# A transformer block on one core: constants issued after the first block's weights, and one pair of weight sums placed behind a block inverse's copies

## The chip, the core and the metric

The kernel runs on one core of a Trainium2 chip. The time is the device time of one execution in microseconds (us); the kernel before has a median of 1452.83 over three runs. A core has engines that work side by side, each in its own order: TensorE (PE in the profile; its weight loads are PEld), VectorE (DVE), ScalarE (ACT), GpSimd (POOL) and SyncE (SP), which here issues loads. Engines wait for one another and for DMA transfers through semaphores.

## The reference

One block of a transformer on x of 256 tokens by 2048:

```python
proj = x @ w_in                                    # 2048 x 11864, split into 12 parts
qkv_a = causal_short_conv(qkv_a, conv_w)           # width 4, then silu
log_decay = -exp(a_log) * softplus(a_in + dt_bias)
o_a = gated_delta_rule_chunked(q_a, k_a, v_a, log_decay, sigmoid(b_in))   # chunks of 64 tokens, triangular solves
o_a = o_a * rsqrt(mean(o_a**2)) * gdn_norm_w * silu(z)
o_b = dsa_sparse_attention(q_b, k_b, v_b, q_i, k_i, w_i, rel_bias)        # top 64 keys by an index score
merged = sigmoid(gate_a) * (o_a @ w_branch_a) + sigmoid(gate_b) * (o_b @ w_branch_b)
x = layer_norm(alpha * x + merged @ w_out)
x = layer_norm(alpha * x + (silu(x @ w_gate) * (x @ w_up)) @ w_ffn_out)
```

## The kernel before

Each float is split into a part hi, rounded to the matmul's format, and a remainder lo, and a product of two floats takes three matmuls (hi by hi, hi by lo, lo by hi). Nearly all of the time is TensorE's work on weights. A weight comes in a chunk of 128 x 1024 floats: `chunk()` (lines 85 to 94) has SP issue the load into `raw` (line 89), ScalarE round it to `hi` (line 91) and VectorE subtract to get `lo` (line 93). `raw`, `hi` and `lo` have four buffers each.

The first block (the loop above line 456) reads x and `win` in eight steps, with a piece of `ws` after every second step (line 454). After the sixth step SP also issued the constants: `ident` and `cp` (an identity matrix, masks and tables; lines 458 and 459), and in a loop (line 462) `cw` (the convolution's taps), `alog`, `dtb`, two parts of `oneh` (shown as s_e, whose memory it shares) and `gnw`. `cw` is first used by the taps of line 480 (ScalarE) and line 482 (VectorE), `cp` and `ident` by products on lines 517 and 521.

Then `wws` is multiplied in groups of four chunks (`group_ws`, lines 153 and 156). After every chunk a clock ticks, and each tick lets chains, which are Python generators, write one more step of other work. TensorE and SP run in exactly this written order. On VectorE, ScalarE and GpSimd a scheduler sets the order when the program is built, from priorities (chunks go ahead by 70 places, `high_priority(offset=lead)`) and the length of the work; when it runs, each engine takes its list strictly from the front.

Two chains matter here. The **block inverse** (`merge`, lines 590 to 640, called for growing blocks) inverts the triangular matrices of the delta rule: products on TensorE (line 606), a copy of each out of PSUM into `s_ak` (VectorE line 610, ScalarE line 612), four groups of four transposes (line 617), each copied into `s_t`, alternately by ScalarE (line 623, groups 0 and 2) and VectorE (line 621, groups 1 and 3), and then products of the two (line 631), which VectorE adds or copies into `s_u` (lines 636 and 638). PSUM has four banks for these small results (`aux`). The **kept pairs** (`kept_chain`) prepare sums of feed-forward weights long before they are needed: for each of four pairs SP issues two loads of 512 KB (line 950), VectorE makes four sums in place (`four_sums`: lines 934, 935, 938, 939), ScalarE casts them to hi (line 960, tile k_hi), VectorE subtracts (line 961), and GpSimd writes both to memory (lines 963 and 964). They have a low priority (`-LEAD`). The pairs alternate between two places, shown as k_rawoh (first and third pair) and k_raws_x (second and fourth); all share one hi buffer. The other work around 200 us is the index score of the sparse attention: ScalarE's relu (line 807, tile rel), VectorE's weighted sums (lines 813 and 815, tile sc), and the search for the largest 64 (lines 822 and 823).

Of the kernel before, what the change touches and what calls it, by code (L numbers as in the profile page):

```python
# [8 lines left out]
F32 = mybir.dt.float32  # L9
# [3 lines left out]
OP = mybir.AluOpType  # L13
# [4 lines left out]
P = 128  # L18
# [14 lines left out]
LEAD = 70  # L33
# [25 lines left out]
C_ID, C_TRI, C_ONE, C_M1, C_M2, C_M3, C_LV, C_SH = 0, 128, 256, 384, 512, 640, 768, 960  # L59
# [4 lines left out]
def block_kernel(ctx: ExitStack, tc: tile.TileContext, xT, x, cpack, onehot, relb, convw, alog, dtb, gnw,  # L64
                 ws, wws, win, wz, wgt, wba, wbb, woa, wob, wfi, wfg, wfo, ln1g, ln1b, ln2g, ln2b, out):
    nc = tc.nc
# [3 lines left out]
    sm = ctx.enter_context(tc.tile_pool(name="sm", bufs=1, side="left"))  # L70
# [4 lines left out]
    def ps_aux():  # L75
        return aux.tile([P, 512], F32, name="aux", tag="aux")
# [4 lines left out]
    ident = cst.tile([P, P], F32, name="ident")  # L81
# [18 lines left out]
    def start(gen, at_once=False):  # L100
        chains.append([gen, clock[0] + (next(gen) if at_once else 0)])
# [17 lines left out]
    def event(name):  # L119
        done[name] = clock[0]  # L120
# [86 lines left out]
    def split(hi, lo, src):  # L207
        nc.scalar.copy(hi, src)
        nc.vector.tensor_sub(lo, src, hi.bitcast(F32))
# [131 lines left out]
    def T(name, shape, dtype=F32, tag=None):  # L341
        return p1.tile(shape, dtype, name=name, tag=tag or name)
# [23 lines left out]
    cp = T("cp", [P, C_N - P])  # L366
    alog_t = T("alog", [P, H])
    dtb_t = T("dtb", [P, H])
    cw = T("cw", [P, 24, 4])
    gnw_t = T("gnw", [P, 1])  # L370
    oneh = s_e.rearrange("p a h d -> p (a h d)")
# [6 lines left out]
    def t16(name):  # L378
        return T(name, [P, NTB, H])
# [46 lines left out]
    def first_chunk(src):  # L426
        raw, hi, lo = (wp.tile([P, 512], d, name=n, tag=n) for n, d in (("raw", F32), ("hi", F32R), ("lo", F32R)))
        hv = [slice(c * S, (c + 1) * S) for c in range(2)]
        for h in hv:
            nc.sync.dma_start(raw[:, h], src[:, h])  # L430
        for c, h in enumerate(hv):
            split(hi[:, h], lo[:, h], raw[:, h])
            ws_mm([pss[c]], hi[:, h], lo[:, h], 0, KT, xh, xl, 2)

    for i in range(8):
        k0 = 2 * i
        parts = [srcs[i]] if i > 2 else [srcs[i][:, :512], srcs[i][:, 512:]]
        for j, src in enumerate(parts):
            k, n = k0 + j, 2 // len(parts)
            xr = xraw[k // 8][:, k % 8:k % 8 + n, :]  # L440
            xp = XH[k // 4][:, k % 4:k % 4 + n], XL[k // 4][:, k % 4:k % 4 + n]
            if i:
                nc.sync.dma_start(xr, xT[:, k:k + n, :])
            if k == 0:
                nc.vector.tensor_copy(xp[0], xr)
                nc.vector.tensor_sub(xp[1], xr, xp[0].bitcast(F32))
                first_chunk(src)
            else:
                split(*xp, xr)
                hi, lo = chunk(src, lead=0)  # L450
                ws_mm(pss, hi, lo, k, KT, xh, xl, 4)
        if i % 2:
            ww = slice((i - 1) * 256, (i + 1) * 256)
            nc.sync.dma_start(wsr[:, ww], ws[i // 2])
            split(wsh[:, ww], wsl[:, ww], wsr[:, ww])
            ws_mm([pk], wsh[:, ww], wsl[:, ww], k0 - 2, KT, xh, xl, 1)
        if i == 5:
            nc.sync.dma_start(ident, cpack[:, C_ID:C_ID + P])
            nc.sync.dma_start(cp, cpack[:, P:])
            for dst, src in ((cw, convw), (alog_t, alog), (dtb_t, dtb), (oneh[:32, :384], onehot),  # L460
                             (oneh[:32, 384:392], relb), (gnw_t, gnw)):
                nc.sync.dma_start(dst, src)

    smT = T("smT", [P, S])
    nc.scalar.copy(smT, pk[:, :S])
# [118 lines left out]

    rk2, rk, nb, nbe, rkb = t16("rk2"), t16("rk"), t16("nb"), t16("nbe"), t16("rkb")
    rq2, rq, fo = t16("rq2"), t16("rq"), t16("fo")
    d_m = dr.tile([4, NTB * H, 32, 32], F32, name="d_m")
    d_x = dr.tile([4, NTB * H, 32, 32], F32, name="d_x")

    def merge(b):  # L590

        n = P // (2 * b)
        hi = (64, P) if n == 1 else (0, P)
        w = 64 if n == 1 else 96
        uv = s_u.rearrange("p t (n two b) -> p t n two b", two=2, b=b)
        if n == 1:
            mp, up = mnv[:, :, 0:64], s_u[:, :, 0:64]
        else:
            mp = s_sq.rearrange("p (t c) -> p t c", c=64)
            up = s_e.rearrange("p a h d -> p (a h d)")[:, 0:1024].rearrange("p (t c) -> p t c", c=64)  # L600
            nc.scalar.copy(up.rearrange("p t (n b) -> p t n b", n=n), uv[:, :, :, 0, :])
        for q in range(2):
            a = ps_aux()
            for i in range(8):
                t = q * 8 + i
                nc.tensor.matmul(a[0:64, i * 64:(i + 1) * 64], mp[hi[0]:hi[1], t, :], uv[hi[0]:hi[1], t, :, 1, :],
                                 start=True, stop=True)
            dst = s_ak[0:64, q * 512:(q + 1) * 512]
            if q % 2:
                nc.vector.tensor_copy(dst, a[0:64])  # L610
            else:
                nc.scalar.copy(dst, a[0:64])
                yield 1
        for q in range(4):
            a = ps_aux()
            for i in range(4):
                nc.tensor.transpose(a[0:64, i * w:(i + 1) * w], up[0:w, q * 4 + i, :], ident[0:w, 0:w])
            dst = s_t[0:64, q * 4:q * 4 + 4, 0:w]
            src = a[0:64, 0:4 * w].rearrange("p (t d) -> p t d", t=4)
            if q % 2:  # L620
                nc.vector.tensor_copy(dst, src)
            else:
                nc.scalar.copy(dst, src)
            if q == 1:
                yield 1
        yield 2
        for q in range(2):
            a = ps_aux()
            for i in range(8):
                t = q * 8 + i  # L630
                nc.tensor.matmul(a[0:w, i * 64:(i + 1) * 64], s_t[0:64, t, 0:w], s_ak[0:64, t * 64:(t + 1) * 64],
                                 start=True, stop=True)
            dst = uv[0:w, q * 8:q * 8 + 8, :, 1, :]
            src = a[0:w].rearrange("p (t n b) -> p t n b", t=8, b=b)
            if n == 1:
                nc.vector.tensor_copy(dst, src)
            else:
                nc.vector.tensor_tensor(dst, src, dst, op=OP.add)
            yield 1 if q == 0 else 3


    def key_chain():
# [54 lines left out]
        yield "qc1s"  # L697
        yield from merge(32)
        yield from merge(64)
        event("inv")  # L700

# [225 lines left out]

    d_s = dr.tile([len(KEPT), 2, P, 2, 1024], F32, name="d_s")

    def four_sums(ra, rb, lead=0):  # L930

        r0, r1, s0, s1 = (t[:, n * 512:n * 512 + 512] for t in (ra, rb) for n in range(2))
        with tc.high_priority(offset=lead):
            nc.vector.tensor_add(r0, r0, s1)
            nc.vector.tensor_add(s1, r1, s1)
        yield 1
        with tc.high_priority(offset=lead):
            nc.vector.tensor_add(r1, r0, r1)
            nc.vector.tensor_add(s0, r1, s0)

    def kept_chain(ms, wait, old, old_hi, gap, ev):
        yield wait
        raws = [T(f"k_raw{t}", [P, 2, 1024], tag=t) for t in old]
        hi = T(f"k_hi{old_hi}", [P, 2, 1024], F32R, tag=old_hi)
        for m in ms:
            if gap and m > ms[0]:
                yield gap
            raw = raws[m % len(old)]
            for i in range(2):
                nc.sync.dma_start(raw[:, i], wfg[KEPT[m] - 1, i])  # L950
                yield 1
            yield 1
            for _ in four_sums(raw[:, 0], raw[:, 1], -LEAD):
                yield 1
            yield 1
            for i in range(2):
                with tc.high_priority(offset=-LEAD):
                    for n in range(2):
                        cs = slice(n * 512, n * 512 + 512)
                        nc.scalar.copy(hi[:, i, cs], raw[:, i, cs])  # L960
                        nc.vector.tensor_sub(raw[:, i, cs].bitcast(F32R), raw[:, i, cs], hi[:, i, cs].bitcast(F32))
                yield 1
                nc.gpsimd.dma_start(d_s[m, 0, :, i], hi[:, i].bitcast(F32))
                nc.gpsimd.dma_start(d_s[m, 1, :, i], raw[:, i])
        event(ev)

    start(kept_chain(range(4), KEPT_FROM, ("oh_", "s_x"), "ol_", 0, "kept0"))
    conv_first(s_kT, pss)
    event("kc0")
# [646 lines left out]
    for j in (1, 2, 3):  # L1616
        nc.vector.scalar_tensor_tensor(v1[j], v1[j], mv[:, 0:1], gt2[:, slice(j * 512, j * 512 + 512)],
                                       op0=OP.subtract, op1=OP.mult)
    for j in (1, 2, 3):
        nc.vector.scalar_tensor_tensor(v1[j], v1[j], rs, bt2[:, slice(j * 512, j * 512 + 512)],  # L1620
                                       op0=OP.mult, op1=OP.add)
# [113 lines left out]
```

## Time and profile before

| What | us |
|---|---|
| Median of three runs (1451.66 to 1455.95) | 1452.83 |
| The profiled execution | 1453.58 |
| its span in the trace | 1451.8 |
| TensorE busy in it | 1443.1 |
| VectorE busy | 1283.2 |
| ScalarE busy | 816.6 |

The difference between the profiled execution's time and its span, 1.78 us, lies around the span. A row of a timeline gives the start, the duration, the engine, the line of the kernel, the operation, what it writes and reads, its shape and how many stand together, and in brackets the idle time of the engine just before it and what ended that. A row of the waits gives engine, tile and line, what was waited for, and the total, the number and the longest wait. Times in both are us from the start of the span.

### The profile page before, as it was taken

How to read it: one execution, taken by the hardware profiler on the slowest of the kernel's cores; microseconds unless marked ns; L12 is line 12 of the kernel's file. 1: busy time of each engine (PE TensorE's matmuls, PEld its weight loads, DVE VectorE, ACT ScalarE, POOL GpSimd, SP SyncE). 2: the span in 40 equal slices, each digit the busy share in tenths (PEclk: the TensorE clock that was granted, in tenths of full speed). 3: DMA queues.
4: the chain of work that ended last, by engine and by line, in shares of the span. 5: the costliest groups of instructions: out<-in, count | busy, mean ns of one | idle time of the engine just before them, and what ended most of it. 6: DMA issues, size and time to landing. Idle time of an engine off the chain costs nothing.

```text
span 1451.8 us, 19648 instructions
## 1 busy us (share of the span) xinstructions
PE 1443.1 (99%) x7137; PEld 1214.2 (84%) x7137; DVE 1283.2 (88%) x1769; ACT 816.6 (56%) x1025; POOL 58.3 (4%) x79
## 2 busy tenths in 40 slices
PE   9999999999999999999999999999999999999998
PEld 8888888888888888888888888888888888888886
DVE  6798988789799969998897899999999998989987
ACT  5765454557556646655445565656566565554552
POOL 0001011121000000000000000000000000000000
PEclk9999999999999999999999999999999999999999
DMA  8656589854456775766865777677766666888863
GB/s 290 196 162 196 174 213 335 287 188 159 171 202 221 264 248 201 249 186 208 296 210 202 244 263 281 244 267 257 279 214 211 213 218 247 313 338 269 318 210 116
DMA packets 102833, 339.81 MB, mean 234 GB/s; under 512 B 17792, under 2 KB 18984, under 8 KB 102224
## 3 DMA queue, kind: packets, MB, share of 16 engines
q1 hardware_dynamic: 88800, 311.35, 62.1%
q0 software_dynamic: 6752, 24.85, 5.0%
q10 hardware_dynamic: 7184, 2.36, 0.7%
q8 instruction: 56, 0.92, 0.3%
q14 instruction: 41, 0.34, 0.1%
HBM read 314.19 MB, written 24.31 MB: 233 GB/s over the span
## 4 chain that ended last, share of the span: by engine, by line
PE 98%; DMA 1%; ACT 0%; DVE 0%; issue 0%; POOLq 0%; SPq 0%; ACTq 0%; DVEq 0%
PE acc L217 11%; PE acc L218 11%; PE acc L219 11%; PE acc L153 10%; PE aux L217 10%; PE aux L219 10%; PE aux L218 10%; PE acc L156 5%; PE acc L173 4%; PE acc L175 4%; PE acc L174 4%; PE aux L174 2%; PE aux L175 2%; PE aux L173 1%; PE aux L737 1%; DMA k_rawoh__2366<-in_wfg_dram 1%
## 5 line engine op out<-in xcount | busy, mean ns | idle before, releaser
L91 ACT CAST hi<-raw 128x1024 fp32r<-128x1024 f32 (+1 forms) x384 | 392.9, 1033 | 326.7 <-PE acc L219 71.7
L93 DVE TENSOR_TENSOR lo<-raw,hi 128x1024 fp32r<-128x1024 f32 (+1 forms) x384 | 458.9, 1205 | 82.4 <-ACT hi L91 78.4
L153 PE MATMUL acc<-X,hi 128*128 128x512 f32 x640 | 203.7, 400 | 0.0
L217 PE MATMUL acc<-hi,X 128*128 128x512 f32 x370 | 145.2, 392 | 0.0
L219 PE MATMUL acc<-hi,X 128*128 128x512 f32 x370 | 144.1, 389 | 0.0
L218 PE MATMUL acc<-lo,X 128*128 128x512 f32 x370 | 144.0, 389 | 0.0
L156 PEld LDWEIGHTS acc<-X,lo 128*128 128x128 f32 x640 | 120.2, 188 | 28.3
L156 PE MATMUL acc<-X,lo 128*128 128x256 f32 x640 | 126.0, 278 | 0.0
L217 PE MATMUL aux<-hi,X 128*128 128x512 f32 x306 | 119.7, 391 | 0.0
L219 PE MATMUL aux<-hi,X 128*128 128x512 f32 x306 | 119.2, 389 | 0.0
L218 PE MATMUL aux<-lo,X 128*128 128x512 f32 x306 | 119.1, 389 | 0.0
L153 PEld LDWEIGHTS acc<-X,hi 128*128 128x128 f32 x640 | 97.5, 189 | 2.0 <-ACT hi L91 0.7
L241 ACT CAST f_thi<-f_wt 128x1024 fp32r<-128x1024 f32 x60 | 63.2, 1053 | 59.7 <-DVE f_wt L246 23.8
L219 PEld LDWEIGHTS acc<-hi,X 128*128 128x128 f32 x370 | 69.4, 188 | 14.5
L217 PEld LDWEIGHTS acc<-hi,X 128*128 128x128 f32 x370 | 69.5, 188 | 14.3 <-ACT s_u L979 0.4
L218 PEld LDWEIGHTS acc<-lo,X 128*128 128x128 f32 x370 | 69.5, 188 | 14.0
L242 DVE TENSOR_TENSOR f_tlo<-f_wt,f_thi 128x1024 fp32r<-128x1024 f32 x60 | 73.1, 1219 | 7.2 <-ACT f_thi L241 7.0
L219 PEld LDWEIGHTS aux<-hi,X 128*128 128x128 f32 x306 | 57.4, 188 | 12.0
L218 PEld LDWEIGHTS aux<-lo,X 128*128 128x128 f32 x306 | 57.5, 188 | 11.9
L217 PEld LDWEIGHTS aux<-hi,X 128*128 128x128 f32 x306 | 57.4, 188 | 11.7
L173 PE MATMUL acc<-hi,X 128*128 128x512 f32 x160 | 64.3, 402 | 0.0
L241 ACT CAST thi<-wt 128x1024 fp32r<-128x1024 f32 x36 | 37.9, 1053 | 46.2 <-DVE wt L246 29.6
(661 smaller groups left out, 3145.1 us busy)
## 6 DMA issues: line engine op xcount, KB each, us to landing
raw<-in_wfg_dram SPq DMA_DIRECT2D x125, 512.0 KB, 5.1
raw<-in_wws_dram SPq DMA_DIRECT2D x80, 512.0 KB, 4.2
raw<-in_wfo_dram SPq DMA_DIRECT2D x70, 512.0 KB, 5.1
raw<-in_wgt_dram SPq DMA_DIRECT2D x49, 512.0 KB, 3.7
f_wraw<-in_wfg_dram SPq DMA_DIRECT2D x30, 512.0 KB, 6.5
raw<-in_win_dram SPq DMA_DIRECT2D x21, 512.0 KB, 4.1
kept<-d_s SPq DMA_DIRECT2D x20, 512.0 KB, 7.7
wraw<-in_wfo_dram SPq DMA_DIRECT2D x18, 512.0 KB, 5.2
```

The source lines that it names most:

```text
L91: nc.scalar.copy(hi, raw)
L93: nc.vector.tensor_sub(lo, raw, hi.bitcast(F32))
L153: nc.tensor.matmul(pss[c], hv[:, kk, cs[c]], X2[k // 4][:, k % 4], start=(k == 0), stop=False, skip_group_check=True)
L156: nc.tensor.matmul(pss[c][:, :S], lv[:, kk, cs[c]], xh[:, k, :], start=False, stop=(k == KT - 1), skip_group_check=True)
L173: nc.tensor.matmul(ps, xh, hv[:, kk], start=(k == 0), stop=False)
L174: nc.tensor.matmul(ps, xh, lv[:, kk], start=False, stop=False)
L175: nc.tensor.matmul(ps, xl, hv[:, kk], start=False, stop=(k == 2 * n - 1))
L217: nc.tensor.matmul(o, sh, hi, start=first, stop=False)
L218: nc.tensor.matmul(o, sh, lo, start=False, stop=False)
L219: nc.tensor.matmul(o, sl, hi, start=False, stop=last)
L241: nc.scalar.copy(hi, v)
L242: nc.vector.tensor_sub(lo, v, hi.bitcast(F32))
```

## The change

First part: the constants leave the first block. `cw` is issued after the block's last load, and the other seven loads become a chain that is started before all others, so its one step is written at the first tick, after the first chunk of `wws`. Second part: a tile `one`, one column of ones, is set at the start (VectorE). The copies into `s_t` on VectorE (groups 1 and 3) become multiplications by `one`. Before the third kept pair's first sum (m == 2) `one` is written again, and that sum becomes a multiply-add, r0 * one + s1. The new write must wait until every earlier reader of `one` has run, so the sum, and what follows from it, comes behind the last copy into `s_t`. What is computed stays the same.

```diff
@@ first block
-        if i == 5:
-            nc.sync.dma_start(ident, cpack[:, C_ID:C_ID + P])
-            nc.sync.dma_start(cp, cpack[:, P:])
-            for dst, src in ((cw, convw), (alog_t, alog), (dtb_t, dtb), (oneh[:32, :384], onehot),
-                             (oneh[:32, 384:392], relb), (gnw_t, gnw)):
-                nc.sync.dma_start(dst, src)
+    nc.sync.dma_start(cw, convw)
+
+    def constants():
+        for dst, src in ((ident, cpack[:, C_ID:C_ID + P]), (cp, cpack[:, P:]), (alog_t, alog), (dtb_t, dtb),
+                         (oneh[:32, :384], onehot), (oneh[:32, 384:392], relb), (gnw_t, gnw)):
+            nc.sync.dma_start(dst, src)
+        yield 1
+
+    start(constants())
@@ before merge
+    one = sm.tile([P, 1], F32, name="one")
+    nc.vector.memset(one, 1.0)
@@ merge
             if q % 2:
-                nc.vector.tensor_copy(dst, src)
+                nc.vector.tensor_scalar(dst, src, one[0:64], None, op0=OP.mult)
             else:
                 nc.scalar.copy(dst, src)
@@ four_sums
-    def four_sums(ra, rb, lead=0):
+    def four_sums(ra, rb, lead, pin):
         r0, r1, s0, s1 = (t[:, n * 512:n * 512 + 512] for t in (ra, rb) for n in range(2))
         with tc.high_priority(offset=lead):
-            nc.vector.tensor_add(r0, r0, s1)
+            if pin is None:
+                nc.vector.tensor_add(r0, r0, s1)
+            else:
+                nc.vector.memset(pin, 1.0)
+                nc.vector.scalar_tensor_tensor(r0, r0, pin, s1, op0=OP.mult, op1=OP.add)
             nc.vector.tensor_add(s1, r1, s1)
@@ kept_chain
-            for _ in four_sums(raw[:, 0], raw[:, 1], -LEAD):
+            for _ in four_sums(raw[:, 0], raw[:, 1], -LEAD, one if m == 2 else None):
```

The lines of the kernel move by 3 to 9 below the change: lines 606, 610, 612, 617, 621, 623, 631 become 611, 615, 617, 622, 626, 628, 636; 934, 935, 938, 939, 960, 961 become 940 (943 for the multiply-add), 944, 947, 948, 969, 970; 813 and 815 become 818 and 820; 480, 482, 746 become 483, 485, 751.

TensorE's order is the same row for row. On SP, the loads around the end of the first block, as a piece of the difference (raw from `win` and s_rv from x are the first block's, raw from `wws` the first group's chunk):

```order
 L454 DMA s_mn<-in_ws_dram 128x512
-L458 DMA ident<-in_cpack_dram 128x128
-L459 DMA cp<-in_cpack_dram 128x960
-L462 DMA cw<-in_convw_dram 128x96
+L443 DMA s_rv<-in_xT_dram 128x512
+L89 DMA raw<-in_win_dram 128x1024
+L443 DMA s_rv<-in_xT_dram 128x512
+L89 DMA raw<-in_win_dram 128x1024
+L454 DMA s_mn<-in_ws_dram 128x512
+L457 DMA cw<-in_convw_dram 128x96
+L89 DMA raw<-in_wws_dram 128x1024
+L462 DMA ident<-in_cpack_dram 128x128
+L462 DMA cp<-in_cpack_dram 128x960
```

The last loads of the first block, cw and the first chunk of `wws` now go ahead of `ident`, `cp` and the five small ones, which keep their order and are followed by the second chunk.

On VectorE at the third kept pair, before (the last step of the block inverse is L610 and L621):

```order
L93 TENSOR_TENSOR lo<-raw,hi 128x1024 x2
L934 TENSOR_TENSOR k_rawoh__2366<-k_rawoh__2366 128x512
L935 TENSOR_TENSOR k_rawoh__2366<-k_rawoh__2366 128x512
L938 TENSOR_TENSOR k_rawoh__2366<-k_rawoh__2366 128x512
L961 TENSOR_TENSOR k_rawoh__2366<-k_rawoh__2366,k_hiol__2368 128x512
L939 TENSOR_TENSOR k_rawoh__2366<-k_rawoh__2366 128x512
L610 COPY s_ak<-aux 64x512
L621 COPY s_t<-aux 64x4x64
L93 TENSOR_TENSOR lo<-raw,hi 128x1024
L961 TENSOR_TENSOR k_rawoh__2366<-k_rawoh__2366,k_hiol__2368 128x512 x2
L621 COPY s_t<-aux 64x4x64
```

And with the change:

```order
L93 TENSOR_TENSOR lo<-raw,hi 128x1024 x2
L615 COPY s_ak<-aux 64x512
L626 TENSOR_SCALAR s_t<-aux,one 64x4x64 x2
L93 TENSOR_TENSOR lo<-raw,hi 128x1024
L942 MEMSET one 128x1
L943 SCALAR_TENSOR_TENSOR k_rawoh__2368<-k_rawoh__2368,one 128x512
L944 TENSOR_TENSOR k_rawoh__2368<-k_rawoh__2368 128x512
L947 TENSOR_TENSOR k_rawoh__2368<-k_rawoh__2368 128x512
L948 TENSOR_TENSOR k_rawoh__2368<-k_rawoh__2368 128x512
```

The three copies of the inverse went from behind the pair's sums to ahead of them, with one lo between. On ScalarE the same holds for the casts of this pair (L960, now L969): they stood ahead of the first L623 and around the second, and now stand behind both L628.

The scheduler built a new order for the first 290 us, so other rows moved too. On VectorE at the first kept pair, before (the rows behind the block of s_rv; sc is the index score; the pair's sums came 18 rows and more below):

```order
L746 TENSOR_TENSOR s_rv<-aux,rkb 128x512 x2
L93 TENSOR_TENSOR lo<-raw,hi 128x1024
L813 TENSOR_SCALAR sc_2124<-rel,smt 128x128
L815 SCALAR_TENSOR_TENSOR sc_2124<-rel,smt,sc_2124 128x128 x4
L93 TENSOR_TENSOR lo<-raw,hi 128x1024
```

And with the change:

```order
L751 TENSOR_TENSOR s_rv<-aux,rkb 128x512 x2
L93 TENSOR_TENSOR lo<-raw,hi 128x1024
L940 TENSOR_TENSOR k_rawoh__2368<-k_rawoh__2368 128x512
L944 TENSOR_TENSOR k_rawoh__2368<-k_rawoh__2368 128x512
L947 TENSOR_TENSOR k_rawoh__2368<-k_rawoh__2368 128x512
L818 TENSOR_SCALAR sc_2126<-rel,smt 128x128
L948 TENSOR_TENSOR k_rawoh__2368<-k_rawoh__2368 128x512
L820 SCALAR_TENSOR_TENSOR sc_2126<-rel,smt,sc_2126 128x128
L93 TENSOR_TENSOR lo<-raw,hi 128x1024
```

The pair's four sums now stand ahead of the next lo. Among the smaller moves on ScalarE are three more table loads before 130 us (15 in all now, 12 before), the second `wws` chunk's hi behind two taps of line 483, and on VectorE that chunk's lo behind five taps of line 485 and one more lo ahead of the first sums of line 686 (now 691).

## The prediction

> **What bounds the kernel now.** I read the page's totals first, then TensorE's waits, then the timelines around the one wait that lies inside the run, and last the stretches in which the change moves work.
>
> ```profile
> PE 1443.1 (99%) x7137; PEld 1214.2 (84%) x7137; DVE 1283.2 (88%) x1769; ACT 816.6 (56%) x1025; POOL 58.3 (4%) x79
> PE 98%; DMA 1%; ACT 0%; DVE 0%; issue 0%; POOLq 0%; SPq 0%; ACTq 0%; DVEq 0%
> PE acc L136 <- ACT hi L91: 1.7, 1, 1.7
> PE aux L421 <- DVE warm L417: 1.1, 1, 1.1
> PE aux L617 <- ACT s_t L623: 0.8, 1, 0.8
> PE aux L1612 <- ACT ct L1606: 0.7, 1, 0.7
> ```
>
> TensorE is busy for 1443.1 of the span's 1451.8 us, and the chain of work that ended last is TensorE for 98%. It idles for 8.7 us in all, and only four waits are long enough to be listed: L421 and L136 at the very start, L1612 at the very end, and L617. Everything that the change touches is loads, VectorE or ScalarE work, so it can act on the time only through idle time of TensorE. Of the idle time only the 0.8 us at L617 can be reached (the wait at L136 is over at 7.78, before any moved load). That caps the gain.
>
> The stall stands in the timelines of TensorE, VectorE and ScalarE, in this order:
>
> ```profile
> 251.73 0.63 PE L617 MATMUL aux<-ident,s_u 64*64 64x64 f32 x8
> 252.29 0.73 PE L153 MATMUL acc<-X,hi 128*128 128x512 f32 x2
> 255.28 0.41 PE L617 MATMUL aux<-ident,s_u 64*64 64x64 f32 x4
> 256.51 0.41 PE L617 MATMUL aux<-ident,s_u 64*64 64x64 f32 x4 [0.81 <-ACT s_t L623]
> 252.60 0.69 DVE L934 TENSOR_TENSOR k_rawoh__2366<-k_rawoh__2366 128x512 f32<-128x512 f32 x1 [3.78 <-DMA k_rawoh__2366<-in_wfg_dram]
> 255.96 0.68 DVE L610 COPY s_ak<-aux 64x512 f32<-64x512 f32 x1
> 256.09 0.36 ACT L623 COPY s_t<-aux 64x256 f32<-64x256 f32 x1
> 243.66 8.85 DMA k_rawoh__2366<-in_wfg_dram
> ```
>
> The last row is from the chain of waits: the second half of the third kept pair was issued at 243.66 and took 8.85 us, to 252.51. Both engines take their work in order. VectorE stood 3.78 us at the pair's first sum, L934, and ran five of the pair's instructions before the block inverse's copy at 255.96, whose input TensorE had finished long before. ScalarE stood at L960, the pair's cast, behind that sum, so its copy of s_t, L623, came only at 256.09. The fourth group of transposes (L617) needs the bank which that copy frees. Eight transposes take 0.56 us from start to start (251.73 to 252.29), so four take 0.28: the fourth group could have begun at 255.56 and began at 256.51. The stall is worth **0.95 us**, and its 0.81 of idle is the lower bound.
>
> **The pin.** The third pair's sums now stand behind the last L621 on VectorE, and L960 behind both L623 on ScalarE. On either engine only copies and lo or hi chunks stand ahead now, none of which waits for that load. By the times above the copies can run at once: s_ak from about 251.8 (the products before it end when the transposes start, 251.73), the first s_t after 252.29, and the fourth group finds its bank free at 255.56. So this removes 0.95 us.
>
> What it adds: two MEMSETs of one column, one multiply-add in place of an addition, and four copies that become multiplications by one. The nearest rows bound them:
>
> ```profile
> 228.14 0.28 DVE L825 TENSOR_SCALAR wk<-wk 128x256 f32<-128x256 f32 x1
> 35.34 0.48 DVE L482 SCALAR_TENSOR_TENSOR s_kT<-acc,cw,s_kT 128x255 f32<-128x255 f32 x1 [0.56 <-ACT s_kT L480]
> 259.23 0.41 DVE L621 COPY s_t<-aux 64x256 f32<-64x256 f32 x1
> 262.62 1.14 PE L631 MATMUL aux<-s_ak,s_t 64*64 64x64 f32 x16
> 275.21 0.69 DVE L934 TENSOR_TENSOR k_raws_x<-k_raws_x 128x512 f32<-128x512 f32 x1 [1.61 <-DMA k_raws_x<-in_wfg_dram]
> ```
>
> The memsets write one column each, far less than any row here; the first lies in VectorE's wait for the first x. The multiply-add takes the addition's place (0.69) in the third pair, off the path. A multiplication of 256 columns costs from 0.28 to 0.48 against the copy's 0.41, so each of the four lies between -0.13 and +0.07; I take the copy's own 0.41, since source and shape are its own. None of it reaches TensorE: L631 takes s_t at 262.62, and the last copy ended at 259.64 even with the stall in front. Without that 3 us of cover it would be 4 x 0.07 = 0.3 us at most. What is late next is the third pair itself: its first sum moves from 252.60 to about 257.6 (the last copy ends near 256.4, then one lo of 1.2), some 5 us. Its last L961 ended at 261.38 and would end near 267, and the fourth pair, which shares the hi buffer, begins at 275.21. Eight us of cover, cost 0.
>
> **The constants.** SP's rows and the first uses:
>
> ```profile
> 13.54 0.65 SPq L458 DMA_DIRECT2D ident<-in_cpack_dram  x1
> 24.61 21.39 SPq L89 DMA_DIRECT2D raw<-in_wws_dram  x10
> 31.18 1.05 ACT L91 CAST hi<-raw 128x1024 fp32r<-128x1024 f32 x1 [0.39 <-DMA raw<-in_wws_dram]
> 32.47 1.05 ACT L91 CAST hi<-raw 128x1024 fp32r<-128x1024 f32 x1 [0.23 <-DMA raw<-in_wws_dram]
> 34.83 0.47 ACT L480 ACTIVATE s_kT<-acc,cw 128x256 f32<-128x256 f32 x1 [1.31 <-PE acc L139]
> 40.05 0.39 PE L156 MATMUL acc<-X,lo 128*128 128x256 f32 x2
> 42.45 0.70 PE L517 MATMUL aux<-smT,cp 64*128 64x256 f32 x2
> ```
>
> Eight loads leave from 13.54 on, before the last pieces of the block. The block's last two x and weight pieces pass them and come earlier, but TensorE does not wait between 11 and 42 us, so the gain is 0. cw, now ahead of the first wws chunk, is there before that chunk, whose cast began at 31.18 although eight loads stood ahead of it; its first use is at 34.83, where ScalarE waited for TensorE anyway. The other seven stand ahead of the second chunk, which carries the same bytes ahead of it as before, so they land no later than it did, and its cast began at 32.47; their first use by TensorE is 42.45. Cover 3.7 and 10 us, cost 0.
>
> The scheduler shifts more: the second chunk's hi now comes behind two taps (L480, from 34.83) on ScalarE, and its lo behind five taps of 0.48 on VectorE. From 35.34 these last to about 37.7, and the lo (1.2) ends near 38.9; TensorE takes it at 40.05. The margin shrinks to 1.1 us, cost 0. ScalarE also gets three more table loads further on:
>
> ```profile
> 44.76 1.28 ACT L488 ACT_TABLE_LOAD   x1
> 127.09 0.16 DVE L686 TENSOR_TENSOR s_e<-s_e 128x2 f32<-128x2 f32 x1 [3.11 <-POOL s_e L683]
> 127.62 1.21 DVE L93 TENSOR_TENSOR lo<-raw,hi 128x1024 fp32r<-128x1024 f32 x1
> 129.31 0.39 PE L156 MATMUL acc<-X,lo 128*128 128x256 f32 x2
> ```
>
> That is 3 x 1.28 = 3.8 us on an engine which is busy for 56% of the span (its share in the first fence). The tightest place there is L686 at 127.09, with 0.5 us between the end of the lo behind it (128.83) and its use at 129.31. In the new order that lo stands ahead of L686 and no longer waits for it; what a later L686 delays is the next one, which TensorE takes a chunk later, 2.8 us. Cost 0, with bounds of 0 and 1.2 us, one lo.
>
> **The first kept pair** moves too, and this speaks against the change:
>
> ```profile
> 191.73 1.22 DVE L93 TENSOR_TENSOR lo<-raw,hi 128x1024 fp32r<-128x1024 f32 x1
> 195.47 0.29 DVE L813 TENSOR_SCALAR sc<-rel,smt 128x128 f32<-128x128 f32 x1 [2.52 <-ACT rel L807]
> 207.10 0.68 DVE L934 TENSOR_TENSOR k_rawoh__2366<-k_rawoh__2366 128x512 f32<-128x512 f32 x1
> L950 SPq DMA_DIRECT2D k_rawoh__2366<-in_wfg_dram x1: 427/427/427, 193.4 to 193.4; - x1
> DMA to landing us min/median/max: 5.9/5.9/5.9
> 204.97 0.39 PE L156 MATMUL acc<-X,lo 128*128 128x256 f32 x2
> ```
>
> Its first sum ran at 207.10; now three of its sums stand directly behind the lo of 191.73, ahead of L813. The second half is issued at 193.4 (the rows of L950 in that stretch) and lands 5.9 us later, at 199.3. So VectorE stands from 192.95 to 199.3. Then come three sums of 0.7, an L813 of 0.3, the fourth sum of 0.6 and one L815 of 0.3: the next lo starts at 202.6 and ends at 203.8. TensorE takes it at 204.97. Margin 1.2 us, cost 0; with the 8.85 us of the third pair's load it would end at 206.7, a stall of 1.7 us.
>
> The sum, against the profiled execution (span 1451.8, 1.78 around it, 1453.58): 1453.58 - 0.95 = 1452.63. That execution lies 0.75 above the median of the three runs, so against the median it is 1452.83 - 0.95 = **1451.9**.
>
> **Rivals.** First: the change does not show. The stall may come back at another wait, since a hi cast still stands ahead of either s_t copy on ScalarE. It would take a cast that runs past 255.2 (the copy takes 0.36). Against it: a cast takes 1.05, and between 252.29 and 255.56 lie 3.3 us. Time 1452.8.
>
> Second, slower: VectorE's stand at the first kept pair outlasts the margin. It decides from a landing time of 5.9 + 1.2 = 7.1 us; this load took 5.9 in the same company, but the third pair's took 8.85. Price 1.7 us, so 1452.83 - 0.95 + 1.7 = 1453.6. A gap of this length has slowed TensorE once:
>
> ```profile
> 7.78 0.58 PE L136 MATMUL acc<-X,hi 128*128 128x256 f32 x1 [1.73 <-ACT hi L91]
> 10.81 0.36 PE L136 MATMUL acc<-X,hi 128*128 128x256 f32 x1
> 7.50:11.00 3.50, 3.22 (x13) 3.00 (x14) 3.14 (x6) 3.02 (x8) 0.00 (x0) 0.51 0.99 357
> 255.00:258.00 3.00, 2.19 (x17) 1.67 (x16) 3.00 (x5) 3.00 (x6) 1.07 (x2) 1.00 0.16 63
> ```
>
> The last two rows are windows; the granted clock is third from the end. It was 0.51 after the idle 1.73 us that ended at 7.78, and 1.00 through the 0.95 us stall. The 3.03 us from 7.78 to 10.81, at 0.51, hold work of 3.03 x 0.51 = 1.55 at full clock: 1.5 us more. With that the time is 1455.1. The Trainium skill's "TensorE: Matmul & The Clock Gate", Part 1, says that the clock halves after an idle window of about 3.4 us; by that rule a 1.7 us gap inside the run costs itself alone, 1453.6. The 0.51 in the row after only 1.73 us of idle speaks against reading the rule so narrowly, though that gap came when TensorE had hardly started.
>
> Third, faster by far: earlier first-block pieces would help if TensorE waited for them; the list of waits has none between 7.78 and 256.51, so I give it next to nothing.
>
> **How the numbers follow.** The stall gone and nothing new: 0.62, at 1451.9. Not showing: 0.17, 1452.8. The first pair late: 0.14, 1453.6 to 1455.1. The remaining 0.07 is for an order I have not priced: a chunk missed once, 2.8 us with or without the slow clock's 1.5, up to 1456. The three runs lie from 1.2 below to 3.1 above their median, so the likeliest case's own range is 1450.4 to 1453.4; with the rivals 1449.9 to 1455.2. A measurement of this kernel tells 0.3%, 4.4 us, from no change: only the worst of the last two cases, with noise, passes it upwards (0.05), and downwards the cap of 0.95 leaves noise alone (0.03). Same: 0.92.
>
> **What would show it.** Right: no L617 (now L622) among TensorE's waits; ScalarE's first s_t copy near 253; the third pair's first sum after the last s_t copy, near 257.6; VectorE idle some 6 us for k_rawoh near 193 to 199, and the lo behind it ended by 204; first use of cw and cp without a wait. Wrong: a wait of TensorE for lo near 205, 130 or 40, a granted clock below 1 there, or TensorE's last matmul of the inverse not about 1 us earlier than before.

## The result: 1.0% slower, with TensorE busy all the way

| | before | changed |
|---|---|---|
| Median of six runs, us | 1453.47 (1451.66 to 1455.95) | 1467.46 (1465.97 to 1472.82) |
| Ratio, 95% interval | | 1.0102 [1.0091, 1.0114] |
| The profiled execution, us | 1453.58 | 1472.82 |
| its span, us | 1451.8 | 1471.0 |

The changed kernel is slower by 14.0 us, and the predicted range ended at 1455.2. Its profiled execution is the longest of its six, 5.4 us above the median, so it shows more loss than a usual run.

The page's totals of the changed kernel, the row that answers to the first of the prediction:

```profile
PE 1458.6 (99%) x7137; PEld 1214.9 (83%) x7137; DVE 1284.2 (87%) x1771; ACT 818.2 (56%) x1028; POOL 59.3 (4%) x79
```

TensorE ran the same 7137 matmuls and was busy 1458.6 us instead of 1443.1. So 15.5 of the 19.2 us by which the span grew lie in time that counts as busy. TensorE's waits in the changed kernel, those of over 1 us (total, number, longest):

```profile
PE acc L217 <- ACT s_u L988: 1.8, 1, 1.8
PE aux L622 <- ACT s_t L628: 1.6, 1, 1.6
PE acc L136 <- ACT hi L91: 1.5, 2, 1.0
PE aux L421 <- DVE one L591: 1.1, 1, 1.1
```

Two of these are new, L217 at 363 us and an L622 at 229 us; neither is the third kept pair's. They are worth 3.4 us. For the rest I compared equal stretches of both kernels. A row of these windows holds the stretch, its length, then busy us and number of instructions of PE, PEld, DVE, ACT and POOL, the granted clock, the DMA share and GB/s. Before:

```profile
1100.00:1200.00 100.00, 100.00 (x451) 82.96 (x450) 95.91 (x115) 60.00 (x72) 2.64 (x5) 1.00 0.63 222
1300.00:1400.00 100.00, 100.00 (x443) 82.81 (x442) 94.13 (x103) 55.99 (x59) 3.15 (x6) 1.00 0.79 279
```

Changed:

```profile
1100.00:1200.00 100.00, 100.00 (x452) 82.46 (x451) 95.17 (x114) 62.24 (x76) 1.59 (x3) 1.00 0.61 211
1300.00:1400.00 100.00, 100.00 (x432) 80.96 (x432) 90.64 (x100) 53.31 (x57) 3.13 (x6) 1.00 0.84 304
```

From 1300 to 1400 TensorE is busy for all 100 us at a granted clock of 1.00 in both, and finishes 432 matmuls instead of 443. From 1100 to 1200 it loses nothing. The groups of the late stretch (the costliest form there, count, busy us and mean ns of one, idle time before it), before:

```profile
L217 PE MATMUL acc<-hi,hH 128*128 128x512 f32 x67 | 26.1, 389 | 0.0
```

Changed:

```profile
L217 PE MATMUL acc<-hi,hH 128*128 128x512 f32 x56 | 22.2, 396 | 0.0
```

The same matmul takes 396 ns instead of 389, with no idle time before it and its order unchanged. (These are durations of single matmuls, which overlap; below I use the time from one start to the next, some 227 ns.) Set against the profiled run of before, matmul by matmul, the changed kernel is 5.6 us late at 372 us and 19.2 us late at the end. The last 13.6 us grow over a thousand us in which no wait of TensorE is listed but the one that before has at the end too. That was the question for the experiments: what makes a matmul of 512 columns slower that the change doesn't touch?

### The profile page after: what moved, and what is told of

Read it like the earlier page. It is cut to its first block, busy times and chain, and to the rows that moved or that the text cites. A ratio compares the mean times of both kernels' runs of the same rounds, so it can differ in the third digit from the quotient of the medians.

```text
span 1471.0 us, 19637 instructions
## 1 busy us (share of the span) xinstructions
PE 1458.6 (99%) x7137; PEld 1214.9 (83%) x7137; DVE 1284.2 (87%) x1771; ACT 818.2 (56%) x1028; POOL 59.3 (4%) x79
## 4 chain that ended last, share of the span: by engine, by line
PE 72%; DVE 1%; DMA 1%; issue 0%; ACT 0%; POOLq 0%; DVEq 0%
PE acc L217 10%; PE acc L219 10%; PE acc L218 10%; PE aux L219 9%; PE aux L217 9%; PE aux L218 9%; PE acc L173 2%; PE acc L175 2%; PE acc L174 2%; PE aux L173 2%; PE aux L174 2%; PE aux L175 2%; DMA raw<-in_wfg_dram 1%; PE aux L1131 0%; PE aux L900 0%
## 5 line engine op out<-in xcount | busy, mean ns | idle before, releaser
L153 PE MATMUL acc<-X,hi 128*128 128x512 f32 x640 | 203.7, 400 | 0.0
L217 PE MATMUL acc<-hi,X 128*128 128x512 f32 x370 | 146.2, 395 | 1.8 <-ACT s_u L988 1.8
L219 PE MATMUL acc<-hi,X 128*128 128x512 f32 x370 | 144.9, 392 | 0.0
L217 PE MATMUL aux<-hi,X 128*128 128x512 f32 x306 | 120.2, 393 | 0.0
L153 PEld LDWEIGHTS acc<-X,hi 128*128 128x128 f32 x640 | 97.5, 189 | 2.0 <-issue 0.7
L217 PEld LDWEIGHTS acc<-hi,X 128*128 128x128 f32 x370 | 69.7, 188 | 17.1 <-ACT s_u L988 2.3
L217 PEld LDWEIGHTS aux<-hi,X 128*128 128x128 f32 x306 | 57.5, 188 | 12.4
L173 PE MATMUL acc<-hi,X 128*128 128x512 f32 x160 | 64.5, 403 | 0.0
L175 PE MATMUL acc<-hi,X 128*128 128x512 f32 x160 | 62.6, 391 | 0.0
```

Of the source, the lines that this page charges most:

```text
L153: nc.tensor.matmul(pss[c], hv[:, kk, cs[c]], X2[k // 4][:, k % 4], start=(k == 0), stop=False, skip_group_check=True)
L173: nc.tensor.matmul(ps, xh, hv[:, kk], start=(k == 0), stop=False)
L175: nc.tensor.matmul(ps, xl, hv[:, kk], start=False, stop=(k == 2 * n - 1))
L217: nc.tensor.matmul(o, sh, hi, start=first, stop=False)
L219: nc.tensor.matmul(o, sl, hi, start=False, stop=last)
```

## The experiments

**The theory and its rivals.** The one thing that the change does to work behind 372 us is to place it elsewhere in memory. The tile `one` has one column, but takes 32 bytes in each partition, and every tile allocated behind it on that side of the on-chip memory lies 32 bytes further on: s_kT moves from address 58752 to 58784, s_vT, whose memory the feed-forward's hH shares, from 75136 to 75168. The chunk buffers (8832 to 53888) and X (from 196480) stay. (These addresses are those the program was built with, not rows of a trace.) In the expectations the theories whose letter is A make this placement the cause: A1 says that data and weights must lie alike within 64 bytes, A2 that any operand off a 64 byte boundary is slow, A3 that 128 bytes restore the pace, A4 that any new tile there costs, because distances of 256 bytes or more count, A5 that the step is 256 bytes. The rivals, B and O, blame the new order: waits early on, or transfers that run at another time.

**e2_before_shift32: the kernel before, with nothing but the addresses moved.** A scratch tile that exists already is made longer; its new columns are never used, and every engine's order is that of before.

```diff
-    warm = sm.tile([P, 1], F32, name="warm")
+    warm = sm.tile([P, 16], F32, name="warm")[:, 0:1]
```

> The kernel before with nothing changed but the size of the tile warm, 16 columns instead of 1, which moves every tile allocated behind it on that side by 32 bytes, as the new tile does in the changed kernel. Orders are those of before, row for row. Theory A: 1791 pairs of moving data and next weights lie at different offsets, as in the changed kernel, and the cadence behind 360 us is 232 ns in the same places: 1453.5 + 13.6 = about 1467 (1464 to 1470). Theory B: no difference to before, 1453.5 (1451.5 to 1455.5).

Measured: 1467.08 against 1453.02, 1.0096 [1.0079, 1.0113], which is the changed kernel's loss. The late stretch of this run:

```profile
1300.00:1400.00 100.00, 100.00 (x433) 80.97 (x432) 93.19 (x102) 54.57 (x59) 3.14 (x6) 1.00 0.83 294
```

433 matmuls, beside 432 in the changed kernel. So moving tiles by 32 bytes is enough for the loss, and neither the order, nor the moved constants, nor the pin is needed for it.

**e1_after_64: the changed kernel, moved by 64 bytes.**

```diff
-    one = sm.tile([P, 1], F32, name="one")
+    one = sm.tile([P, 16], F32, name="one")[:, 0:1]
```

> The changed kernel with its one column of ones in a tile of 16 columns (64 bytes) instead of 1 (32 bytes as placed). Every engine's order is the same as in the changed kernel, row for row; only the addresses of the tiles behind it differ: they lie 64 bytes further than before the change, not 32. Theory A (addresses): in the changed kernel the float32r matmuls of 512 columns start 232 ns apart, not 227, wherever the moving data and the next weights lie at different offsets within 64 bytes (1200 of 0 against 32 alone cost 7.4 us of the 13.6 us lost behind 372 us); here all lie at 0 again, so the cadence is 227 and the time falls by 13.6 us from 1467.5 to about 1454 (1452.5 to 1456). Theory B (order): the loss comes from the new order of VectorE and ScalarE; nothing of it changes here, so 1467 (1465 to 1470).

Measured: 1466.58 against 1453.02, 1.0095 [1.008, 1.011]. The expectation fell: 64 bytes don't restore the pace. By itself this is also what theory B, the order, forecasts; e2 rules that out.

**e3_left_shift32 and e4_all_shift32: which tiles must stay together.** Both are the kernel before. e3 lengthens the first tile of that side, so that all of it moves by 32 bytes, the chunk buffers too, while X stays; e4 does that and lengthens a tile on X's side.

```diff
-    ident = cst.tile([P, P], F32, name="ident")
+    ident = cst.tile([P, P + 8], F32, name="ident")[:, :P]
-    pad = padp.tile([P, 24], F32, name="pad")            # e4 alone
+    pad = padp.tile([P, 32], F32, name="pad")[:, :24]    # e4 alone
```

> The kernel before with the first tile, ident, 8 columns wider: every tile on the left side moves by 32 bytes, the chunks' raw, hi and lo too, while the tiles on the right side (X2, the split x) stay. Orders as before. If what counts is that moving data and next weights differ in their offset within 64 bytes (theory A1), 4273 pairs differ, 3400 of them with 512 columns moving: 3400 x 6.1 ns = 21 us, or 26 us if those with 256 columns pay too, so 1474 to 1480, with the loss in the places where chunks meet X2, from the start of the run on. If any operand off a 64 byte boundary is slow whatever the other is (A2), it is 5476 x 6 ns = 33 us, 1486. Theory B: 1453.5.

> As e3, and the first tile on the right side is 32 bytes wider too, so that X2 moves as well: all matmul operands lie at offset 32 within 64 bytes. Orders as before. A1 (the difference counts): no pair differs but 2, so 1453.5 (1451.5 to 1456). A2 (the offset itself counts): the slowest of all, 5476 matmuls of 512 columns x 6 ns = 33 us, 1486. Theory B: 1453.5.

Measured: e3 1472.45, 1.0133 [1.0118, 1.0148]; e4 1458.15, 1.0034 [1.0021, 1.0047]. e4 was meant to move everything alike, but that side is filled from the top, so X went down by 32 bytes, and the two sides came to stand 64 bytes apart. The windows of e3:

```profile
1100.00:1200.00 100.00, 100.00 (x444) 81.03 (x444) 93.71 (x112) 59.47 (x73) 1.58 (x3) 1.00 0.62 207
1300.00:1400.00 100.00, 100.00 (x442) 82.55 (x441) 90.93 (x99) 53.23 (x57) 3.14 (x6) 1.00 0.86 309
```

The loss has changed places. From 1100 to 1200, where data of the chunk buffers mostly stream past weights taken from X, e3 finishes 444 instead of 451, and the changed kernel lost nothing. From 1300 to 1400, where hH and the chunk buffers meet and in e3 have moved together, e3 is at 442, while the changed kernel was at 432. So it is not an address that matters, but how two operands lie to each other. (By A1 I had 1474 to 1480 for e3; it came out a little below.)

**The measure.** For every pair of float32r matmuls of 512 columns behind 372 us that follow each other without a gap, I took the time from start to start out of the trace, and from the built program the distance from the address of the first one's moving data to that of the second one's weights, modulo 256 bytes. Mean, median and number of pairs (before, the changed kernel and those runs that tell something new; e5 to e12 follow below):

```
distance   kernel      mean ns   median   pairs
   0       before       226.9     227     4524
  32       changed      233.3     234      319
  32       e3           233.4     234     2482
  64       e1           228.6     229      319
  64       e4           229.1     229     2481
 128       e5, e7       233.4     232     1647 (each)
 128       e8           232.6     232     2480
 192       e1           232.9     233     1328
 224       changed, e2  233.1     232     1328 (each)
   0       e9 to e12    226.9     227     4520 (about, each)
```

In before every distance is 0: all operands of these matmuls lie 128 bytes behind a multiple of 256. At other distances a matmul of 227 ns takes some 2 to 6.5 ns more. In the changed kernel the 1647 pairs that went from 0 to 32 or 224 cost 6.2 ns each, 10.2 of the 13.6 us. Another 3.5 us lie in the 2875 pairs that stayed at 0, whose mean went to 228.1 with a median still at 227: the 198 of them that stand directly behind a pair at another distance take 232.1, and those more than 30 matmuls away from any take 226.8 (226.9 in before). Because the pair behind a slow one is slow too, the table doesn't settle whether the distance to the next weights alone sets the pace.

**e5_after_128, e7_pin_only_128, e8_all_phase32: is 128 the step?** e5 is the changed kernel, e7 the kernel before with the pin alone (the constants as before); both give `one` 32 columns, which moves the tiles by 128 bytes. e8 is e4 with the padding longer, so that the two sides stand 128 bytes apart.

```diff
+    one = sm.tile([P, 32], F32, name="one")[:, 0:1]      # e5, e7
+    pad = padp.tile([P, 48], F32, name="pad")[:, :24]    # e8, beside the longer ident
```

> The changed kernel with its column of ones in a tile of 32 columns, so that the tiles behind it lie 128 bytes further than before the change. Orders are those of the changed kernel, row for row. With 64 bytes the cadence behind 372 us still cost 12.0 us, so 64 was not the measure. Theory A3: what counts is the offset within 128 bytes of moving data against next weights; here all pairs are equal again, the cadence is that of before, and only what the order does is left: -0.95 at the third pair, +2.3 at 224 to 229, up to +3.4 at 361, so 1455.5 (1453 to 1458.5). Rival A4: any tile of any size there costs 12 us, because other distances count (256 bytes or more): 1466 to 1468.

> The kernel before with the second part alone (the column of ones, the multiplications, the pin at the third pair), the column in a tile of 32 columns (128 bytes). The constants stay in the first block. VectorE's list has the first pair's sums in the middle of the index score, as before. Theory A3 with theory O: the stall at the third pair is gone and nothing else changes, 1453.0 - 0.95 = 1452.1 (1450.5 to 1453.5). If the pin itself brings the loss in the order: 1455 or more. If A4 holds: 1465.

> As the run in which all tiles were moved, but with X2 moved down by 96 bytes instead of 32: every operand of a 512 column matmul now lies at offset 32 within 128 bytes (there X2 lay at 96 against 32, and those pairs cost 2.3 ns). Orders as before. If only the difference within 128 bytes counts (A3): 1453 (1451.5 to 1455). If an offset counts for itself: 1458 or more, as in that run.

Measured: e5 1468.21 against 1453.74, 1.0097 [1.0083, 1.0111]; e7 1467.09, 1.0090 [1.0076, 1.0104]; e8 1470.66, 1.0114 [1.0101, 1.0128]. All three keep the loss, and A3 falls. e5's windows repeat the changed kernel's pattern:

```profile
1100.00:1200.00 100.00, 100.00 (x451) 82.28 (x450) 95.12 (x116) 60.91 (x75) 1.59 (x3) 1.00 0.61 211
1300.00:1400.00 100.00, 100.00 (x432) 80.83 (x431) 91.13 (x99) 54.47 (x58) 3.13 (x6) 1.00 0.83 298
```

**e9_after_256, e10_pin_only_256, e11_all_diff0: 256.** e9 is the changed kernel and e10 the pin alone, both with `one` of 64 columns, which moves the tiles by 256 bytes. e11 is before with the two sides moved so that every operand lies 32 bytes behind its old place modulo 256, and every distance is 0 again.

```diff
+    one = sm.tile([P, 64], F32, name="one")[:, 0:1]      # e9, e10
+    pad = padp.tile([P, 80], F32, name="pad")[:, :24]    # e11, beside the longer ident
```

> The changed kernel with its column of ones in a tile of 64 columns: the tiles behind it lie 256 bytes further than before the change; orders are those of the changed kernel. Over all runs so far the start-to-start time of a 512 column matmul follows the distance from its moving data to the next weights within 256 bytes: 227 ns at 0, 233 at 32, 229 at 64, 233 at 128, 192 and 224. Theory A5 (256 bytes): all distances are 0 again, the cadence is that of before, and only the order's own part is left, +1.5 to +2.5 by the stalls near 224 to 229 and 361 less the 0.95 at the third pair: 1455.5 (1453.5 to 1457.5). Theory A4 (any tile there costs): 1467.

> The second part alone with the column of ones in a tile of 64 columns (256 bytes). A5: cadence as before; the stall at the third pair gone, as it was with 128 bytes (no wait for s_t among TensorE's waits); nothing else: 1453.7 - 0.95 = 1452.8 (1451.3 to 1454.2). A4: 1466.

> The kernel before with all left tiles 32 bytes up and X2 224 bytes down, so that every operand lies 32 bytes from where it was within 256, and every distance between moving data and weights is again a multiple of 256. Orders as before. A5: 1453.7 (1452 to 1455.5). If an operand's own offset counts: 1470, as with all tiles moved but distances of 128 between chunks and X2.

Measured, against 1453.69: e9 1454.23, 1.0004 [0.9995, 1.0012]; e10 1453.50, 0.9997 [0.9989, 1.0006]; e11 1453.51, 0.9999 [0.9990, 1.0008]. The loss is gone in all three. e9's order is the changed kernel's row for row, and its late stretch reads:

```profile
1300.00:1400.00 100.00, 100.00 (x443) 82.84 (x442) 94.72 (x103) 55.99 (x59) 3.12 (x6) 1.00 0.79 281
```

443 again. e9 against the changed kernel shows that the loss is the placement; e11 shows that the distance decides, since each of its addresses is off the old grid by 32 bytes.

**e12_pin_in_warm: the pin without any tile moved.** `one` becomes the second column of the scratch tile that exists already, within the 32 bytes which that takes.

```diff
-    warm = sm.tile([P, 1], F32, name="warm")
+    warm2 = sm.tile([P, 2], F32, name="warm")
+    warm, one = warm2[:, 0:1], warm2[:, 1:2]
```

> The second part alone with the column of ones as the second column of the tile warm, which has room for it: no tile moves at all. Orders as in the run with the pin alone. A5: the same as there, 1452.8 (1451.3 to 1454.2), since a distance of 256 and none should be alike.

Measured: 1453.82 against 1453.69, 1.0001 [0.9992, 1.0010]. The pin is free, and gains nothing that can be told. Its trace shows where the 0.95 us went. TensorE at the third pair and a hundred us later:

```profile
251.50 0.63 PE L619 MATMUL aux<-ident,s_u 64*64 64x64 f32 x8
255.05 0.63 PE L619 MATMUL aux<-ident,s_u 64*64 64x64 f32 x8
359.47 0.50 PE L217 MATMUL acc<-hi,X 128*128 128x512 f32 x1 [1.43 <-ACT s_u L985]
```

The third and fourth group of transposes now stand together, eight in 0.63 us, and the stall is gone; from 250 to 258 TensorE gains 1.00 us on the run of before. At 359.47 it waits for s_u, which it had not done before. ScalarE and VectorE ahead of that, in e12:

```profile
356.88 0.62 ACT L208 CAST g_form<-z_wt 128x512 fp32r<-128x512 f32 x1 [2.18 <-DVE z_wt L314]
358.83 0.59 ACT L985 COPY s_u<-acc 128x512 f32<-128x512 f32 x1
349.00:359.00 10.00, 9.04 (x48) 7.29 (x46) 9.93 (x22) 7.82 (x16) 0.00 (x0) 1.00 0.58 200
```

And in before:

```profile
358.57 0.59 ACT L979 COPY s_u<-acc 128x512 f32<-128x512 f32 x1
359.21 0.50 PE L217 MATMUL acc<-hi,X 128*128 128x512 f32 x1
```

In before s_u ends at 359.16 and TensorE takes it at 359.21: a tie, which no list of waits shows. In e12 TensorE comes earlier, but s_u ends at 359.42, because ScalarE's casts there wait for VectorE, which is busy for 9.93 of the 10 us up to 359 (third number with a count in the window), as in before. So the gain turns into a wait of 1.43 us. e10 has the same wait, 1.2 us.

**e6_consts_only: the constants without the pin and without a new tile.**

```diff
-        if i == 5:
-            nc.sync.dma_start(ident, cpack[:, C_ID:C_ID + P])
...
+    nc.sync.dma_start(cw, convw)
...
+    start(constants())
```

> The kernel before with the first part alone: the constants behind the first block's weights, no tile of ones, no pin. No address moves. VectorE's list then has the first kept pair's sums directly behind the lo ahead of the index score, as in the changed kernel, and the third pair's sums ahead of the block inverse's copies, as before. If the early first pair is what costs time in the order (theory O): VectorE stands for the load near 193 to 201, TensorE waits for lo and s_t near 224 to 229 (+2.3), the 0.95 us stall at the third pair stays, and perhaps +3.4 at 361: 1453 + 2.3 to 5.7 = 1455.3 to 1458.7. If that place is harmless: 1453 (1451.5 to 1454.5).

Measured: 1455.58 against 1453.74, 1.0010 [1.0001, 1.0020]: 1.8 us or 0.1% slower, with an interval from 0.1 to 2.9 us. That lies in theory O's range, but not by its waits: none near 224 to 229 or at 361 is listed. Without the pin the third pair's stall stays, and here it is longer (the last row is a window behind it):

```profile
256.06 0.41 PE L620 MATMUL aux<-ident,s_u 64*64 64x64 f32 x4 [1.51 <-ACT s_t L626]
252.16 0.69 DVE L937 TENSOR_TENSOR k_rawoh__2366<-k_rawoh__2366 128x512 f32<-128x512 f32 x1 [4.49 <-DMA k_rawoh__2366<-in_wfg_dram]
256.90:260.30 3.40, 3.40 (x12) 2.93 (x12) 3.40 (x6) 1.38 (x4) 0.99 (x2) 0.50 0.92 288
```

VectorE stood 4.49 us at the pair's first sum (3.78 in before), and TensorE idled 1.51 us behind it (0.81 in before). Then the granted clock (third from the end) was 0.50 for 3.4 us. From 250 to 262 us TensorE falls 2.3 us behind before's run, 0.7 by the longer stall and the rest at the lower clock. That is one execution; whether the other ten lose their time there was not recorded. No kernel of the twelve beats before by more than its interval.

## Why the prediction was wrong

**The step that failed** is the one that limited everything else: "Everything that the change touches is loads, VectorE or ScalarE work, so it can act on the time only through idle time of TensorE", and with it "That caps the gain" as a frame for losses too. Under "What it adds" I priced the new memsets, multiplications and the multiply-add, and those prices hold; I gave no price to the tile `one` as a place in memory. It moved operands of matmuls by 32 bytes and changed TensorE's pace while it was busy, a term of +14 us that the sum didn't contain and that no rival named (e2 makes it with nothing else changed, and e9 takes it away with everything else kept). The 0.07 for "an order I have not priced" was for waits, up to 1456, and doesn't cover it either. The range, too, was narrower than its working: a spread from 1.2 below to 3.1 above the median gives 1450.7 to 1455.0 for the likeliest case, not 1450.4 to 1453.4. The measured time lies outside both.

**The pin** was right at its place. L617's wait is gone, and TensorE won 1.0 us there against the 0.95 of the sum. In the changed kernel, where the earlier delay puts these rows some 3 us later, the groups of four stand together as well:

```profile
258.31 0.64 PE L622 MATMUL aux<-ident,s_u 64*64 64x64 f32 x8
258.99 0.48 DVE L626 TENSOR_SCALAR s_t<-aux,one 64x256 f32<-64x256 f32 x1 [2.08 <-PE aux L622]
260.65 0.75 DVE L943 SCALAR_TENSOR_TENSOR k_rawoh__2368<-k_rawoh__2368,one 128x512 f32<-128x512 f32 x1
```

The sum stands behind the last copy into s_t. The multiplication takes 0.48 where I took the copy's 0.41 and had 0.48 as the upper bound; the multiply-add takes 0.75 against the addition's 0.69. Both are covered. "What is late next" failed: I named the third pair's own sums with eight us of cover, and what was late next was s_u at 359. My first rival, that the stall "may come back at another wait", described it, but with a hi cast of the same inverse as its place, and with 0.17 for its chance.

**The constants.** Their first uses cost nothing, as priced: no wait of TensorE for cw, cp or ident is listed in any run.

**The first kept pair** was the second rival, a load that outlasts the margin. Here is VectorE's stand in the changed kernel:

```profile
201.15 0.69 DVE L940 TENSOR_TENSOR k_rawoh__2368<-k_rawoh__2368 128x512 f32<-128x512 f32 x1 [7.51 <-DMA k_rawoh__2368<-in_wfg_dram]
204.27 1.22 DVE L93 TENSOR_TENSOR lo<-raw,hi 128x1024 fp32r<-128x1024 f32 x1
224.48 0.50 PE L156 MATMUL acc<-X,lo 128*128 128x256 f32 x2 [0.31 <-DVE lo L93]
227.53 1.04 ACT L91 CAST hi<-raw 128x1024 fp32r<-128x1024 f32 x1 [2.61 <-DMA raw<-in_wws_dram]
228.48 0.47 ACT L628 COPY s_t<-aux 64x384 f32<-64x384 f32 x1
229.00 0.52 PE L622 MATMUL aux<-ident,s_e 96*64 96x96 f32 x4 [1.59 <-ACT s_t L628]
```

VectorE idled 7.51 us where I had 6.3 (192.95 to 199.3). The lo behind the sums ended at 205.49, 1.7 us after my 203.8, and TensorE did not wait for it. The price came later: between 224 and 229 TensorE falls 2.3 us further behind before's run. There a cast waited 2.61 us for its chunk's load, the copy of s_t stood in the queue behind that cast, and TensorE stood at L622. So the size of the rival (1.7 us) was near by luck, and its place was wrong. That the late chunk comes from the stand at the first pair is not shown: in e6 VectorE stands at the same place for 6.12 us, and TensorE doesn't wait at L622. Waits of 1.4 to 1.9 us at the same L622 stand in e1, e5 and e9, which carry both parts of the change too, and none stands there in e6, e7, e10 and e12, which carry one part each.

With the placement put right (e9), the order as a whole comes out at 1.0004 [0.9995, 1.0012]: no change that can be told. The 0.95 us of the likeliest case lie just outside this interval, which ends 0.7 us below before. In e9's trace TensorE loses 1.6 us near 225, gains 1.0 at the third pair and loses 1.4 at 359; I had placed only the gain.

## What to carry to other kernels

A new tile has a cost beyond its instructions: it moves every tile allocated behind it, so compare the operands' addresses before and after as you compare the order of instructions, and put a small new tile into a tile that exists (e12), or round them up to a step that keeps the distances (256 bytes here, e9). Where an engine is busy for 99% and the time still moves, count its instructions in equal stretches of both traces: 443 against 432 at the same granted clock said at once that no wait was to be looked for. A stall that is taken away is worth what the next tie leaves of it, so look along the path for operands that come just in time, which no list of waits shows.

## What the runs showed of the hardware that I had not expected

**The pace of a matmul goes by the distance of two operands.** By the table above, a float32r matmul of 512 columns takes 226.9 ns from start to start where the distance from its moving data to the next matmul's weights is a multiple of 256 bytes, about 229 ns at 64, and 232 to 234 ns at 32, 128, 192 and 224. No other distance was tried. What in the chip does this was not shown; that the weights of the next matmul are loaded while this one's data stream in (PEld is busy for 83% beside PE's 99%) makes a conflict of the two reads a natural guess, no more. Not every matmul follows it: the 512-column matmuls of L153 in the first 350 us, which alternate with 256-column ones and already take some 233 ns, lost nothing at 224 (e3) or 128 (e8), while the 256-column ones lost some 2.8 ns each in e3.

**Gaps of 1.5 to 1.9 us halved the clock in four runs, and one of 1.59 didn't.** In the changed kernel's profiled execution, TensorE at the new wait for s_u, and three windows, around the 1.59 us gap at 229, behind the 1.83 us gap, and after that; the last two rows are e1's wait at L622 and a window behind it:

```profile
363.15 0.50 PE L217 MATMUL acc<-hi,X 128*128 128x512 f32 x1 [1.83 <-ACT s_u L988]
223.00:231.00 8.00, 6.09 (x41) 5.00 (x40) 8.00 (x19) 4.81 (x8) 0.00 (x0) 1.00 0.96 293
363.60:367.00 3.40, 3.40 (x14) 2.90 (x13) 1.74 (x7) 2.05 (x3) 0.00 (x0) 0.50 0.46 155
367.00:371.00 4.00, 4.00 (x19) 3.29 (x18) 2.09 (x3) 1.05 (x1) 0.00 (x0) 1.00 0.38 125
226.83 0.66 PE L622 MATMUL aux<-ident,s_e 96*64 96x96 f32 x4 [1.90 <-ACT s_t L628]
227.10:230.50 3.40, 3.40 (x14) 2.92 (x12) 3.40 (x9) 1.53 (x4) 0.00 (x0) 0.50 1.01 352
```

The granted clock is third from the end: 0.50 for 3.4 us from shortly after TensorE had resumed, then 1.00 again. It cost about 1.5 us, the size that the prediction's second rival had for such a stretch, and it may be part of why this execution is the longest of its six. The same came behind the gap of 1.90 in e1, of 1.51 in e6 (its window stands there) and of 1.73 at the start of before. The gaps of 1.59 here, 1.43 in e12, and 1.42 and 1.38 in e9 left the clock at 1.00. So a gap far below 3.4 us can halve it, but the length alone doesn't decide: 1.51 did and 1.59 did not. The Trainium skill's "TensorE: Matmul & The Clock Gate", Part 1, has the half rate follow an idle window of about 3.4 us and end after a busy one of the same length; the length of the slow stretch agrees, the idle time before it does not, and these few cases fix no threshold.
